# A streaming encoder layer on one core: two-input elementwise work of the input phase and of the up-projection's weights moved from GpSimd to VectorE, with a new table for the middle's steps

## The chip, the cores and the metric

The kernel runs on one core of a Trainium2 chip. The metric is the device time of one execution in microseconds (us), the median of several runs. Five engines work side by side, each taking its own queue of instructions in order: TensorE (PE; its weight loads are listed as PEld), VectorE (DVE), ScalarE (ACT), GpSimd (POOL) and SyncE (SP), which here only issues DMA transfers. ACT and POOL issue transfers as well, in order with their other instructions.

## The reference

One layer of a streaming encoder is computed for 1024 new prompt frames and 32 frames that continue an older stream, 1056 tokens with a model width of 1024, all in float32:

```python
proj = x @ prm['w_in']
q_lat, kv_lat, k_rope_raw, u, p_rwkv = jnp.split(proj, IN_SPLITS, axis=-1)
mla_out, ckv, krope = mla_mixer(q_lat, kv_lat, k_rope_raw, pos, ...)    # 6 heads, chunk-causal
s5_out, s5_state = s5_mixer(u, s5_x0, s5_block_len, prm)                 # 16 groups, 64 complex states
rwkv_out, rwkv_state, shift = rwkv_mixer(p_rwkv, shift0, rwkv_s0, prm)   # 6 heads of 64
merged = jnp.concatenate([mla_out, s5_out, rwkv_out], -1)
x = layer_norm(ALPHA * x + merged @ prm['w_out'], prm['ln1_g'], prm['ln1_b'])
hidden = jnp.square(jax.nn.relu(x @ prm['w_up']))                        # 4096 wide
x = layer_norm(ALPHA * x + hidden @ prm['w_down'], prm['ln2_g'], prm['ln2_b'])
```

RWKV mixes each token with the one before it, `p + (prev - p) * mu_shift`, ahead of everything else. Attention uses a rotary part of 32 dimensions, and S5 needs powers of a complex diagonal and products with its input and output matrices.

## The kernel before

**Split products.** Each float32 operand of a matrix product is split in two parts. ACT copies it to a rounded high part (L49), and another engine subtracts that from the operand, which leaves the low part, the residue (L50); both are in `split3`. `mm3` then does three products, high by high (L63), high by low (L65) and low by high (L67). The argument `lo_eng` of `split3` and `load3` names the engine of L50; without it, it is VectorE.

**Input phase** (0 to about 283 us). The projection goes in tiles of 128 columns. `load_w` loads the 128x1024 weights of a tile and splits them (`wmraw`, `wmhi`, `wmlo`). For the RWKV columns, `raw_in` has ACT copy the projected tile out of PSUM to `raw`, with GpSimd filling the borders (L222 to L224, L229, L230); `mixed` then makes the token shift: a subtraction of neighbours (L238) and a multiply-add on VectorE (L239). `stage_mixed` passes the shifted tile on, for q = 0 after a product with cumulated decays (helper at L344), otherwise by a DMA that ACT issues; `stage_lora` does the same for its tile (L249 is the issue) and splits the activated tile (`lact`, `lah`, `lal`). `stage_s5_params` computes powers and the products `cl`, `bl`, `tb` (L514 to L531); L538 on PE transposes `bl`, and ACT's copies of L539 follow it. `front_k` normalises and scales the keys of three pairs of heads (L383 to L394, with products at L342, L344 and one with `at` at L388) and hands them to a set of small products and transposes (L727 to L740). `rwkv_inv` makes a triangular inverse in steps on VectorE (L761, L762). `stage_kr` makes the rotary key (L162 to L164); `stage_q` takes the query's products out of PSUM on ACT (L1161), and `attn_setup` prepares tiles for the attention, among others four 32x1056 areas set to zero (L1111).

**Middle** (about 283 to 720 us). Four streams of steps are recorded in turn: F (scores and row maxima), O (exponentials and the product with the values), S (the RWKV scan) and X (S5). Which stream records its next step is read from `PLAN`, a string of 527 letters. Steps keep this order on PE.

**Output projection and first layer norm** (about 700 to 805 us), then the **MLP**. The up-projection (about 805 to 1160) uses seven products of halves in place of eight for each of 16 blocks of weights: sums of weight quarters (`ws`, L1609 and, for the first two blocks, L1762) are split by `operand` into 128x512 parts (`wo`), and sums of the activations (`xr`, `xt`, L1723) into `xo`. VectorE adds the results out of PSUM (L1634). The down-projection (about 1160 to 1450) loads the hidden layer back and splits it on VectorE and ACT.

**What sets the order.** The code is recorded in program order; a scheduler then orders each engine's instructions by a simulated timeline, in which priorities and the table above hold. So where an instruction changes its engine, its place among the others, and theirs, is set anew.

Of the kernel before, what the change touches and what calls it, by code (L numbers as in the profile page):

```python
# [11 lines left out]
ALU = mybir.AluOpType  # L12
# [84 lines left out]
def load_w(g, src, tag, cols):  # L97

    pool = g.wpools.get(tag, g.wpool)
    raw, hi, lo = (pool.tile([P, cols], dt, tag=t, name=tag + x, bufs=n)  # L100
                   for x, dt, (t, n) in zip(("raw", "hi", "lo"), (F32, F32R, F32R), g.wtags.get(tag, ((tag, WB),) * 3)))
    load3(g, src, raw, hi, lo, g.nc.gpsimd)
    return hi, lo


# [46 lines left out]
def stage_kr(g):  # L152

    nc = g.nc
    rope = g.p1.tile([P, T], F32, tag="f", name="ropek", bufs=5)[0:64]
    nc.sync.dma_start(out=rope, in_=g.a["rope"][0:64])
    kc = g.p1.tile([P, T], F32, tag="f", name="krc", bufs=5)
    t = g.p1.tile([P, T], F32, tag="f", name="krt", bufs=5)
    ps = in_proj(g, g.a["w_kr"], "wm", 64)
    for b, (s, n) in enumerate(BLK):  # L160
        nc.scalar.activation(out=kc[0:64, s:s + n], in_=ps[b][0:64, :n], func=AF.Copy)
    nc.gpsimd.tensor_tensor(out=t[0:32], in0=kc[32:64], in1=rope[32:64], op=ALU.mult)  # L162
    nc.gpsimd.tensor_tensor(out=kc[0:32], in0=kc[0:32], in1=rope[0:32], op=ALU.mult)
# [70 lines left out]
def mixed(g, raw, mtile):  # L234

    nc = g.nc
    mix = g.rawp.tile([P, WSH], F32, tag="mix", name="mix", bufs=2)
    nc.gpsimd.tensor_tensor(out=mix, in0=raw[:, 0:WSH], in1=raw[:, 1:WSH + 1], op=ALU.subtract)  # L238
    nc.vector.scalar_tensor_tensor(out=mix, in0=mix, scalar=g.vec[:, V_MU + mtile:V_MU + mtile + 1], in1=raw[:, 1:WSH + 1], op0=ALU.mult, op1=ALU.add)  # L239
    return mix  # L240


def stage_mixed(g, p, q, after=None, w=None):

    mix = mixed(g, raw_in(g, 4 + 3 * p + q, 3 * q + p, after, w), 3 * q + p)
    if q == 0:
        front_tools(g, p)[1](mix, mix, g.cs65[:, p], 1, 4, eng=g.nc.gpsimd)
    else:
        g.nc.scalar.dma_start(out=g.rw_d[p][:, 3] if q == 2 else g.mx_d[p], in_=mix)  # L249

# [6 lines left out]
def stage_lora(g):  # L257

    nc = g.nc
    mix = g.lmix  # L260
    act = g.lq.tile([P, WSH], F32, tag="lact", name="lact", bufs=1)
    g.table = [nc.scalar.activation(out=act[0:32], in_=mix[0:32], func=AF.Tanh)]
    nc.scalar.activation(out=act[32:64], in_=mix[32:64], func=AF.Copy)
    g.table.append(nc.scalar.activation(out=act[64:128], in_=mix[64:128], func=AF.Sigmoid))
    ah = g.lq.tile([P, WSH], F32R, tag="lah", name="lah", bufs=1)
    al = g.lq.tile([P, WSH], F32R, tag="lal", name="lal", bufs=1)
    split3(g, act, ah, al, nc.gpsimd)
    wl = g.lq.tile([P, 384], F32, tag="wl", name="wl", bufs=1)
# [12 lines left out]
    for p in PAIRS:
        cs = slice(p * P, p * P + P)
        nc.gpsimd.memset(g.cs65[:, p, 0:1040].rearrange("p (c x) -> p c x", x=65)[:, :, 0:1], 0.0)
        nc.gpsimd.memset(g.cs65[:, p, 1040:1041], 0.0)
        nc.gpsimd.memset(g.at[:, p, 1024:1026], 0.0)
        for s, n in runs:
            pool, tag = ((g.pfs, "fs"), (g.pt, "pt"))[i % 2]
            i += 1
            w, a = (pool.tile([P, 512], F32, tag=tag, name=tag)[:, :n] for _ in range(2))
            low(w, slice(0, 32), s, n)  # L290
            low(a, slice(32, 64), s, n)
            g.table.append(nc.scalar.activation(out=g.at[:, p, s:s + n], in_=a, func=AF.Sigmoid, bias=g.vec[:, V_A0 + p:V_A0 + p + 1]))
            out, w = (g.cs65[:, p, 1041:1073], w) if n == 32 else (chunk65(g.cs65[:, p], s // 64, n // 64, 1), w.rearrange("p (c x) -> p c x", x=64))
            g.table.append(nc.scalar.activation(out=out, in_=w, func=AF.Sigmoid, bias=g.vec[:, V_W0 + p:V_W0 + p + 1]))
    for p in PAIRS:
        cs = slice(p * P, p * P + P)
        gt = g.lq.tile([P, WSH], F32, tag="o", name="gt", bufs=2)
        nc.gpsimd.memset(gt[:, 1024:1026], 0.0)
        for s, n in runs:
            pool, tag = ((g.pfs, "fs"), (g.pt, "pt"))[i % 2]  # L300
            i += 1
            gate = pool.tile([P, 512], F32, tag=tag, name=tag)[:, :n]
            mm = low(gate, slice(64, 128), s, n)
            nc.vector.tensor_copy(out=gt[:, s:s + n], in_=gate)
        nc.sync.dma_start(out=g.rw_d[p][:, 5, :], in_=gt)
    g.last_lora = mm.ins
# [57 lines left out]
def front_k(g, p):  # L364
# [42 lines left out]
def bc(ap, shape):  # L407
    return ap.broadcast_to(shape)


def stage_s5_params(g, sp):
# [88 lines left out]
    def v4(t):  # L500
        return t[:, :2048].rearrange("p (g l c) -> p g l c", l=L5, c=16)
# [24 lines left out]
    for j in range(7):  # L526
        s3j = [P, G5, 16]
        l = 6 - j
        V.tensor_tensor(out=blv[:, :, j], in0=bbv[0], in1=bc(pr[:, :, l:l + 1], s3j), op=ALU.mult)
        nc.gpsimd.tensor_tensor(out=tbv[:, :, j], in0=bbv[1], in1=bc(pis[:, :, l:l + 1], s3j), op=ALU.mult)  # L530
    V.tensor_tensor(out=blv[:, :, 0:7], in0=blv[:, :, 0:7], in1=tbv[:, :, 0:7], op=ALU.add)  # L531
    V.tensor_copy(out=blv[:, :, 7], in_=bbv[0])
    yield
# [555 lines left out]
def attn_setup(g):  # L1089
# [16 lines left out]
    for i in range(NKT):  # L1106
        for ks in (g.kh, g.kl):
            if i:
                nc.gpsimd.tensor_copy(out=ks[i][64:128], in_=ks[0][64:128])
        for x in g.q2[i] if i < 2 else ():  # L1110
            nc.gpsimd.tensor_tensor(out=x[96:128], in0=g.ckv[96:128], in1=g.ckv[96:128], op=ALU.subtract)  # L1111
# [211 lines left out]
def middle(g, scan):  # L1323
# [36 lines left out]


PLAN = (
    "FFFFFFFFFFFSFFFFSFFFFFFFSFFFFFSFFFFSOOOSOFSOOOSFOOSOOOOSFSSOSOOFOOFSOOSXFOOOSFFOOOOSXOOFOOFSSOSSSOSO"
    "OFFXFXFOSOFOSSXFFFFOOSOSFOSXOSSFSOSOFOFSXOOSOFOSXOSOFOSOFOOXOFOSFSXOOOFSFOSOOOXFSOOSFOSOOXFSOOSFFFFS"
    "FXSFFFFSFFXSOOSFOSOOFSOOOOXFSXSSOOFOSOOSOFXOOSOOOFOSXOSFSOOOSFOOSXOOOOSFOSOXSFOOFXSSSFFFFFFSFSOOXSOS"
    "FFXSSOOFOSOOOSOOXOSOOOOOFSFOOSXSOOFOOOSSXFOSOFSFOFXOOSOFSOSOOFXOOOSSFOFSXFFFSFFFSFFFXSFSFFFSXOOFOSOO"
    "SOOSXSOOFOFSOSXOOFOSOFSOXOSOSFOXSOOOFOSOOOOFSSOSOXFSOOOSFOXFOOSOXSOOSFSSFFFFSFFFOOOOOSOOSOSOOOSOOOSS"
    "OOSSOOSOSOFOOSOOOOOOOOOOOOO"
)


# [1024 lines left out]
```

## Time and profile before

| | |
|---|---|
| median of 3 runs | 1492.15 us (1492.04 to 1496.15) |
| profiled execution, its time | 1493.61 us |
| its span, first to last instruction | 1491.8 us |
| mean granted clock of PE | 0.967 |
| PE busy | 1393.6 us (93%) |
| DVE busy | 960.8 us (64%) |
| ACT busy | 638.5 us (43%) |
| POOL busy | 419.3 us (28%) |

The profile shows one execution. An engine's busy share is a mean over stages that differ much, so times are read by stage: a table of windows gives each engine's busy time in a stretch, and the granted clock of PE in it (1.00 is full speed). A list of waits names, for an engine's idle time, the instruction that ended it. The chain that ended last is followed back from the last instruction, at each step to what released it. A row of a group gives busy us, mean ns of one instruction, and the idle time just before them. All times in windows and timelines count from the span's start.

### The profile page before, as it was taken

Reading aid. Unit: us, or ns where it says so; the run is one execution under the profiler, and the core shown is the slowest. Engines: PE = TensorE matmul, PEld = TensorE weight load, DVE = VectorE, ACT = ScalarE, POOL = GpSimd, SP = SyncE. Lnnn points to the kernel's source line nnn. Section 1 sums busy time; section 2 is a strip of 40 time slices with the busy share of each in tenths; the row PEclk is TensorE's granted clock in tenths of the full one; section 3 lists DMA queues with packets and bytes.
Section 4 is the critical chain, followed back from the end, with each engine's and each line's share of the span. In section 5 each row is a group of like instructions: output and inputs, shape, how many; then the busy total and the mean of one; then the engine's idle time right before and its main releaser. Section 6 shows DMA issues by size and latency. Waiting matters only on the chain.

```text
span 1491.8 us, 28327 instructions
## 1 busy us (share of the span) xinstructions
PE 1393.6 (93%) x11527; PEld 1245.1 (83%) x11527; DVE 960.8 (64%) x1594; ACT 638.5 (43%) x1122; POOL 419.3 (28%) x447
## 2 busy tenths in 40 slices
PE   7899989789999989979899899999999999999996
PEld 6889879567767656656588899999999999999996
DVE  8566859955566745454757875555556687675476
ACT  4434543414645654443324454444445433434332
POOL 3813581511111110121541644444440000000023
PEclk9999999979999999989999899999999999999998
DMA  5234363564343230132543353434428886354231
GB/s 198 88 117 175 102 204 88 144 136 94 90 104 77 79 83 23 40 97 83 185 144 121 100 187 135 156 132 143 159 102 322 305 284 189 102 157 141 68 99 75
DMA packets 150326, 198.59 MB, mean 133 GB/s; under 512 B 53392, under 2 KB 98116, under 8 KB 149688
## 3 DMA queue, kind: packets, MB, share of 16 engines
q1 hardware_dynamic: 129396, 175.91, 37.1%
q10 hardware_dynamic: 20448, 19.88, 4.3%
q8 instruction: 90, 1.47, 0.4%
q0 software_dynamic: 352, 1.01, 0.2%
q14 instruction: 40, 0.33, 0.1%
HBM read 129.42 MB, written 67.28 MB: 132 GB/s over the span
## 4 chain that ended last, share of the span: by engine, by line
PE 70%; DVE 12%; DMA 5%; issue 4%; ACT 4%; POOL 2%; SPq 1%; ACTq 0%; DVEq 0%; POOLq 0%
PE acc L63 17%; PE acc L65 17%; PE acc L67 17%; PE av L1256 3%; DVE y L762 2%; DVE tmp L761 1%; DMA wo<-in_w_out 1%; DMA mraw<-mg_d 1%; PE sc L63 1%; PE st L63 1%; PE st L65 1%; DVE mx L1227 1%; PE st L67 1%; PE prw L883 1%; PE scv L1138 1%
## 5 line engine op out<-in xcount | busy, mean ns | idle before, releaser
L63 PE MATMUL acc<-xo,wo 128*128 128x272 f32 (+1 forms) x896 | 256.3, 287 | 7.3 <-ACT wo L49 5.5
L67 PE MATMUL acc<-xo,wo 128*128 128x256 f32 (+1 forms) x896 | 254.2, 285 | 1.1 <-POOL wo L50 1.1
L65 PE MATMUL acc<-xo,wo 128*128 128x272 f32 (+1 forms) x896 | 254.6, 285 | 0.0
L67 PE MATMUL acc<-hop,wo 128*128 128x272 f32 (+1 forms) x896 | 193.9, 283 | 0.0
L63 PEld LDWEIGHTS acc<-xo,wo 128*128 128x128 f32 x896 | 169.7, 189 | 8.4 <-ACT wo L49 5.9
L67 PEld LDWEIGHTS acc<-xo,wo 128*128 128x128 f32 x896 | 169.4, 190 | 1.3 <-POOL wo L50 1.3
L65 PEld LDWEIGHTS acc<-xo,wo 128*128 128x128 f32 x896 | 170.0, 190 | 0.0
L65 PE MATMUL acc<-hop,wo 128*128 128x272 f32 (+1 forms) x768 | 158.6, 284 | 0.0
L63 PE MATMUL acc<-hop,wo 128*128 128x256 f32 (+1 forms) x768 | 158.3, 284 | 0.0
L67 PEld LDWEIGHTS acc<-hop,wo 128*128 128x128 f32 x896 | 142.7, 188 | 0.0
L63 PE MATMUL acc<-xh,wmhi 128*128 128x384 f32 (+3 forms) x384 | 129.0, 336 | 8.8 <-ACT xh L49 8.0
L65 PE MATMUL acc<-xl,wmhi 128*128 128x384 f32 (+3 forms) x384 | 128.7, 335 | 2.3 <-DVE xl L50 2.1
L67 PE MATMUL acc<-xh,wmlo 128*128 128x384 f32 (+3 forms) x384 | 128.5, 335 | 0.0
L65 PEld LDWEIGHTS acc<-hop,wo 128*128 128x128 f32 x768 | 119.2, 188 | 0.0
L63 PEld LDWEIGHTS acc<-hop,wo 128*128 128x128 f32 x768 | 118.1, 188 | 0.0
L50 POOL TENSOR_TENSOR wo<-ws,wo 128x512 fp32r<-128x512 f32 x64 | 89.6, 1402 | 98.6 <-ACT wo L49 97.4
L2134 POOL TENSOR_TENSOR wr<-wr,gb 128x512 f32<-128x512 f32 (+1 forms) x14 | 19.8, 1436 | 338.3 <-ACT wr L2132 327.2
L49 ACT ACTIVATE wo<-wr 128x512 fp32r<-128x512 f32 (+1 forms) x64 | 47.0, 739 | 119.4 <-PE acc L67 69.9
L50 POOL TENSOR_TENSOR wo<-wr,wo 128x512 fp32r<-128x512 f32 x48 | 66.1, 1380 | 92.7 <-ACT wo L49 92.7
L1256 PE MATMUL av<-ptk,vo 128*128 128x512 f32 (+5 forms) x204 | 75.6, 456 | 12.3 <-POOL ptk L1283 5.6
L1634 DVE TENSOR_TENSOR hx<-acc,u 128x272 f32<-128x272 f32 (+1 forms) x96 | 40.8, 428 | 71.4 <-PE acc L67 71.3
L63 PEld LDWEIGHTS acc<-xh,wmhi 128*128 128x128 f32 (+1 forms) x384 | 72.5, 189 | 12.2 <-ACT xh L49 8.3
(545 smaller groups left out, 3296.2 us busy)
## 6 DMA issues: line engine op xcount, KB each, us to landing
hraw<-h_d SPq DMA_DIRECT2D x48, 528.0 KB, 3.7
wr<-in_w_up SPq DMA_DIRECT2D x35, 512.0 KB, 3.7
h_d<-hx SPq DMA_DIRECT2D x16, 792.0 KB, 3.3
h_d<-ht SPq DMA_DIRECT2D x16, 792.0 KB, 9.6
wd<-in_w_dn SPq DMA_DIRECT2D x16, 512.0 KB, 9.1
wr<-in_w_dn SPq DMA_DIRECT2D x16, 512.0 KB, 5.2
ld<-rw SPq DMA_DIRECT2D x24, 320.0 KB, 4.6
wmraw<-in_w_m SPq DMA_DIRECT2D x12, 512.0 KB, 4.7
```

The source lines that it names most:

```text
L49: nc.scalar.activation(out=hi, in_=ps, func=AF.Copy)
L50: (lo_eng or nc.vector).tensor_tensor(out=lo, in0=ps, in1=hi.bitcast(F32), op=ALU.subtract)
L63: nc.tensor.matmul(out=outs[i], lhsT=lh, rhs=rhs[i][0], start=start, stop=False, **kw)
L65: nc.tensor.matmul(out=outs[i], lhsT=lh, rhs=rhs[i][1], start=False, stop=False, **kw)
L67: nc.tensor.matmul(out=outs[i], lhsT=ll, rhs=rhs[i][0], start=False, stop=stop, **kw)
L761: V.tensor_tensor(out=tv, in0=bc(y[:, :, 0:m, s:s + 1], [H, 2, m, n]), in1=bc(nn[:, :, s:s + 1, s + 1:32], [H, 2, m, n]), op=ALU.mult)
L762: V.tensor_tensor(out=y[:, :, 0:m, s + 1:32], in0=y[:, :, 0:m, s + 1:32], in1=tv, op=ALU.add)
L883: nc.tensor.matmul(out=pw[hsl(c), p - p0, h], lhsT=g.xt[p][hsl(c), t, h], rhs=r[hsl(c), p, K_A:K_NV + 1:K_NV, h], start=True, stop=True)
L1138: nc.tensor.matmul(out=ps[:n, j], lhsT=c, rhs=g.wkv[:, 1, p * P:p * P + P], start=True, stop=True)
L1256: nc.tensor.matmul(out=po[:, c:n], lhsT=vo[:w, kt].rearrange("p a x -> p (a x)")[:, 64 * i:64 * i + P], rhs=pt[:w, c:n], start=kt == tiles ...
L1634: V.tensor_tensor(out=to(c), in0=st.bank[key, c], in1=other(c), op=ALU.add)
L2134: nc.gpsimd.tensor_tensor(out=o[:n, c], in0=o[:n, c], in1=g.gb2[:n, 0, c], op=ALU.mult)
```

## The change

GpSimd's instructions with two inputs in the input phase and for the weights of the up-projection become VectorE's: the residue of each projection weight, of the LoRA tile and of each operand of the up-projection, the subtraction of the token shift, the product of `stage_mixed`, the product at L388, the three of the rotary key and the two lines of S5. The four areas set to zero at L1111, a subtraction of a tile from itself on GpSimd, become a copy by ACT with scale 0. The table of the middle has the same letters in the same numbers (217 O, 140 F, 132 S, 38 X), many of them a few places off. GpSimd keeps the borders of `raw`, its memsets, casts and transfers, and its part of the middle and of the other stages.

```diff
@@ load_w
-    load3(g, src, raw, hi, lo, g.nc.gpsimd)
+    load3(g, src, raw, hi, lo)
@@ stage_kr
-    nc.gpsimd.tensor_tensor(out=t[0:32], in0=kc[32:64], in1=rope[32:64], op=ALU.mult)
-    nc.gpsimd.tensor_tensor(out=kc[0:32], in0=kc[0:32], in1=rope[0:32], op=ALU.mult)
-    nc.gpsimd.tensor_tensor(out=kc[0:32], in0=kc[0:32], in1=t[0:32], op=ALU.add)
+    nc.vector.tensor_tensor(out=t[0:32], in0=kc[32:64], in1=rope[32:64], op=ALU.mult)
+    nc.vector.tensor_tensor(out=kc[0:32], in0=kc[0:32], in1=rope[0:32], op=ALU.mult)
+    nc.vector.tensor_tensor(out=kc[0:32], in0=kc[0:32], in1=t[0:32], op=ALU.add)
@@ mixed
-    nc.gpsimd.tensor_tensor(out=mix, in0=raw[:, 0:WSH], in1=raw[:, 1:WSH + 1], op=ALU.subtract)
+    nc.vector.tensor_tensor(out=mix, in0=raw[:, 0:WSH], in1=raw[:, 1:WSH + 1], op=ALU.subtract)
@@ stage_mixed
-        front_tools(g, p)[1](mix, mix, g.cs65[:, p], 1, 4, eng=g.nc.gpsimd)
+        front_tools(g, p)[1](mix, mix, g.cs65[:, p], 1, 4, eng=g.nc.vector)
@@ stage_lora
-    split3(g, act, ah, al, nc.gpsimd)
+    split3(g, act, ah, al)
@@ front_k
-    nc.gpsimd.tensor_tensor(out=kk, in0=kk, in1=a, op=ALU.mult)
+    nc.vector.tensor_tensor(out=kk, in0=kk, in1=a, op=ALU.mult)
@@ stage_s5_params
-    nc.gpsimd.tensor_tensor(out=v4(tb), in0=bc(csw[:, :, None, :], s4), in1=bc(pis[:, :, :, None], s4), op=ALU.mult)
+    nc.vector.tensor_tensor(out=v4(tb), in0=bc(csw[:, :, None, :], s4), in1=bc(pis[:, :, :, None], s4), op=ALU.mult)
-        nc.gpsimd.tensor_tensor(out=tbv[:, :, j], in0=bbv[1], in1=bc(pis[:, :, l:l + 1], s3j), op=ALU.mult)
+        nc.vector.tensor_tensor(out=tbv[:, :, j], in0=bbv[1], in1=bc(pis[:, :, l:l + 1], s3j), op=ALU.mult)
@@ attn_setup
-            nc.gpsimd.tensor_tensor(out=x[96:128], in0=g.ckv[96:128], in1=g.ckv[96:128], op=ALU.subtract)
+            nc.scalar.activation(out=x[96:128], in_=g.ckv[96:128], func=AF.Copy, scale=0.0)
@@ PLAN (first of its six rows)
-    "FFFFFFFFFFFSFFFFSFFFFFFFSFFFFFSFFFFSOOOSOFSOOOSFOOSOOOOSFSSOSOOFOOFSOOSXFOOOSFFOOOOSXOOFOOFSSOSSSOSO"
+    "FFFFFFFFFFFSFFFFFFSFFFFFFSFFFFSFFFFSOOOSOFSOOOSFOOSOOOOSFSSOSFOOOOFSOOSXFOOOSFOOSXOOOOFFOOOSFSSSOSSO"
...
@@ operand
-    split3(g, src, w[:, 0], w[:, 1], g.nc.gpsimd)
+    split3(g, src, w[:, 0], w[:, 1])
```

What this does to the order of the queues is shown at three places; a row names the line, the operation, output and inputs, and the shape.

The first is on VectorE in the input phase, where the third token shift of the first stretch (L239) and the S5 product `bl` (L531) are made. Before:

```order
L239 SCALAR_TENSOR_TENSOR mix<-mix,vec,raw 128x1058
L597 TENSOR_TENSOR u_94<-u_94,nrm 128x32
L516 TENSOR_TENSOR cl<-cl,tb 128x2048
L521 TENSOR_SCALAR pis<-pi,sgn 128x128
L239 SCALAR_TENSOR_TENSOR mix<-mix,vec,raw 128x1058
L531 TENSOR_TENSOR bl<-bl,tb 128x16x7x16
L239 SCALAR_TENSOR_TENSOR mix<-mix,vec,raw 128x1058 x2
```

The same place now, with `wmlo` the residue of a projection weight and `lal` that of the LoRA tile:

```order
L50 TENSOR_TENSOR wmlo<-wmraw,wmhi 128x1024
L238 TENSOR_TENSOR mix<-raw 128x1058
L565 COPY a_219<-w_753 128x16
L567 COPY u_94<-a_219 128x16
L530 TENSOR_TENSOR tb<-bb,pis 128x256 x7
L50 TENSOR_TENSOR lal<-lact,lah 128x1058
L239 SCALAR_TENSOR_TENSOR mix<-mix,vec,raw 128x1058
L566 TENSOR_SCALAR u_94<-a_219,sgn 128x16
L531 TENSOR_TENSOR bl<-bl,tb 128x16x7x16
L238 TENSOR_TENSOR mix<-raw 128x1058
```

What stood in GpSimd's queue (the residues, L238, L530) stands between VectorE's own instructions, and L516 has moved ahead of this piece.

The second is on ACT at the end of the input phase, among the query's copies out of PSUM (`scq`). Before:

```order
L1161 ACTIVATE qrope<-scq 128x384 x2
L1161 ACTIVATE qturn<-scq 128x384
L1161 ACTIVATE qrope<-scq 128x288
L1161 ACTIVATE qturn<-scq 128x384
L1079 ACTIVATE cpast<-sct 128x512
```

The same place now:

```order
L1161 ACTIVATE qrope<-scq 128x384 x2
L1161 ACTIVATE qturn<-scq 128x384
L1111 ACTIVATE qh<-ckv 32x1056
L1111 ACTIVATE ql<-ckv 32x1056
L1111 ACTIVATE qh<-ckv 32x1056
L1111 ACTIVATE ql<-ckv 32x1056
L1161 ACTIVATE qturn<-scq 128x384
L1161 ACTIVATE qrope<-scq 128x288
```

The four zeroings stand together between two of the copies.

The third is on VectorE at the start of the up-projection, up to the last of the weight sums of the first two blocks (`ws<-ws,wr`) and the first sum out of PSUM (`u<-acc,u`). Before:

```order
L50 TENSOR_TENSOR xo<-xt,xo 128x4x256
L1723 TENSOR_TENSOR xt<-xr,xt 128x1088
L1762 TENSOR_TENSOR ws<-wr 128x512
L1723 TENSOR_TENSOR xt<-xr,xt 128x1024
L1762 TENSOR_TENSOR ws<-wr,ws 128x512
L1762 TENSOR_TENSOR ws<-ws,wr 128x512
L50 TENSOR_TENSOR xo<-xt,xo 128x4x272
L1634 TENSOR_TENSOR u<-acc,u 128x272
```

The same place now, where `wo` are residues of weights:

```order
L50 TENSOR_TENSOR xo<-xt,xo 128x4x256
L1723 TENSOR_TENSOR xt<-xr,xt 128x1088
L50 TENSOR_TENSOR wo<-ws,wo 128x512 x3
L1723 TENSOR_TENSOR xt<-xr,xt 128x1024
L50 TENSOR_TENSOR wo<-wr,wo 128x512 x2
L1762 TENSOR_TENSOR ws<-wr,ws 128x512
L1762 TENSOR_TENSOR ws<-ws,wr 128x512
L1634 TENSOR_TENSOR u<-acc,u 128x272
```

Five residues stand in this piece ahead of the last sum; five more stand ahead of it earlier in the queue, and the residue `xo` of the activations has moved behind `u`.

More of the change, by code (lines that the diff above doesn't have):

```diff
@@ L1362 @@
 PLAN = (
-    "FFFFFFFFFFFSFFFFSFFFFFFFSFFFFFSFFFFSOOOSOFSOOOSFOOSOOOOSFSSOSOOFOOFSOOSXFOOOSFFOOOOSXOOFOOFSSOSSSOSO"
[L1364 to L1368, printed above, removed]
+    "FFFFFFFFFFFSFFFFFFSFFFFFFSFFFFSFFFFSOOOSOFSOOOSFOOSOOOOSFSSOSFOOOOFSOOSXFOOOSFOOSXOOOOFFOOOSFSSSOSSO"
+    "OFFXXFOSFOFOSSXFFFFOOSOSSFOSXOOSFSFSOOFSXOOSOFOSXOSFOOSOOFOFXOXOSFSOOOFSFFOOSOOXSSOOOFSOOXFSFOOSFFFS"
+    "FXSFFFFSFFXSOOSFOSOOFSOOOOXFSSSOOXFOSOOSFXOOSOOOFOOSXOSSOFOOFOSOSXOOOOSFOSOXOFFSOXSFFSSFFFSFFSOOXSOS"
+    "FFXSSFOSOOOOOSOOXOSOOOFOOSFOOSXSFOOOOOSSXFOSFFOOSFOOSXOFSOOSFXOOOOSSFOFSXFFFSFFFSFFFXSFSFFFSOXOFOOSO"
+    "SOOSOXOSFFOSOSOXOFSOOFSOOXOSSXOSOOOOFOFOOOSFSSSOXSOFOOOSFOXFOXOSOSOOSFSSFFFFSFFFOOOOOOSOOSOOSOOOSOSS"
+    "OOSSSOOSOFOSOOOOOOOOOOOOOOO"
 )
```

## The prediction

> **What bounds the kernel now.** The page comes first: its span and its busy times.
>
> ```profile
> span 1491.8 us, 28327 instructions
> PE 1393.6 (93%) x11527; PEld 1245.1 (83%) x11527; DVE 960.8 (64%) x1594; ACT 638.5 (43%) x1122; POOL 419.3 (28%) x447
> ```
>
> TensorE (PE) is busy 93% of the span, so the change can be worth something only where PE is not running, or runs at half clock. GpSimd (POOL), which loses work here, has 28%. The table of windows tells the stages apart. Its columns are the window, its length, the busy time of PE, PEld, VectorE (DVE), ScalarE (ACT) and POOL, the granted clock, the DMA share and GB/s.
>
> ```profile
> 31.00:69.00 38.00, 36.61 (x226) 35.13 (x224) 25.24 (x28) 13.32 (x21) 32.27 (x27) 1.00 0.24 84
> 73.30:76.60 3.30, 3.30 (x13) 3.08 (x11) 1.26 (x1) 1.91 (x5) 2.00 (x2) 0.50 0.73 209
> 182.50:189.20 6.70, 5.79 (x79) 5.26 (x80) 6.67 (x7) 4.34 (x8) 1.53 (x2) 0.50 0.73 172
> 298.60:315.50 16.90, 13.70 (x96) 10.18 (x96) 8.78 (x22) 1.37 (x3) 5.18 (x6) 0.50 0.88 198
> 300.00:725.00 425.00, 381.69 (x4030) 285.47 (x4029) 232.93 (x505) 190.91 (x398) 63.26 (x129) 0.93 0.33 87
> 834.50:844.60 10.10, 7.22 (x31) 6.93 (x32) 10.10 (x11) 2.68 (x5) 8.36 (x5) 0.50 0.47 158
> 850.00:1150.00 300.00, 300.00 (x2476) 300.00 (x2476) 174.24 (x277) 136.56 (x199) 122.93 (x94) 1.00 0.44 161
> 1200.00:1250.00 50.00, 50.00 (x414) 50.00 (x413) 41.94 (x42) 20.74 (x26) 0.00 (x0) 1.00 0.81 269
> ```
>
> In the up-projection (850 to 1150) PE is busy 300 of 300 us at full clock: nothing there can get shorter. In the input phase POOL works 32.27 us out of 38, and there, around 300 and around 840, the granted clock falls to 0.50 after PE has stood still. Work done in such a window takes twice its time, so a window that goes is worth at most half its length.
>
> Next, the groups of instructions: the moved forms on POOL, and like forms on DVE, ACT for the zeroing. The columns are count, total busy time, mean ns of one, then idle time before them.
>
> ```profile
> L50 POOL TENSOR_TENSOR wo<-ws,wo 128x512 fp32r<-128x512 f32 x64 | 89.6, 1402 | 98.6 <-ACT wo L49 97.4 <-PE acc L67 1.3
> L50 POOL TENSOR_TENSOR wmlo<-wmraw,wmhi 128x1024 fp32r<-128x1024 f32 x14 | 34.9, 2490 | 45.0 <-ACT wmhi L49 44.6 <-POOL kpast L1103 0.4
> L50 DVE TENSOR_TENSOR wo<-wr,wo 128x1024 fp32r<-128x1024 f32 x16 | 19.6, 1224 | 15.0 <-ACT wo L49 15.0
> L1206 ACT ACTIVATE qh<-kh 32x1056 fp32r<-32x1056 f32 x4 | 4.3, 1079 | 0.1
> ```
>
> The same subtraction of 128x1024 takes 2490 ns on POOL and 1224 on DVE: about 1.2 ns for each element of a row. From that I estimate 1.27 us for a 1058-wide operation on DVE, 2.3 for 2048, 0.65 for 512 and 0.4 for 256.
>
> **Part by part. The first stall (T1, 55 to 77 us).** Waits, the chain that ended last, and DVE's timeline:
>
> ```profile
> PE pt L538 <- ACT em L539: 2.6, 1, 2.6
> PE pt L538 <- DVE bl L531: 1.2, 1, 1.2
> ```
>
> ```profile
> 57.37 2.40 POOL lal L50
> ...
> 59.84 3.55 POOL raw L224
> 63.39 2.32 POOL wmlo L50
> ...
> 69.24 0.33 ACTq L249
> ...
> 71.63 1.15 PE pt L538 x8
> ```
>
> ```profile
> 52.11 1.69 DVE L239 SCALAR_TENSOR_TENSOR mix<-mix,vec,raw 128x1058 f32<-128x1058 f32 x1 [4.45 <-POOL mix L238]
> 57.40 5.96 DVE L531 TENSOR_TENSOR bl<-bl,tb 128x1792 f32<-128x1792 f32 x1 [3.60 <-POOL tb L530]
> 67.89 1.32 DVE L239 SCALAR_TENSOR_TENSOR mix<-mix,vec,raw 128x1058 f32<-128x1058 f32 x1 [4.52 <-POOL mix L238]
> ```
>
> The third token shift of this stretch (L238, then L239 on DVE) comes last in POOL's row of work, and DVE starts its half only at 67.89. ACT can't issue the DMA of that tile (L249) before, and the copy of L539, for which PE waits, stands behind that issue in ACT's queue. L531 (5.96 us from 57.40) and the one-column copy of L224 (3.55 from 59.84) lie beside each other: the copy has next to nothing to do and waits for L531, which itself waits for lal. The Trainium skill, page "SBUF — State Buffer", section "Who interferes with whom", says that a DVE instruction with two SBUF inputs and a GpSimd one that reads SBUF exclude each other for the whole instruction, and these two rows agree.
>
> Between 50.2 and 67.9 DVE now has L239 (1.7), two L238 (2.5), seven L530 (2.8), lal (1.3), L531 alone (1792 wide, 2.0), one wmlo (1.2): 11.5 us for what took 17.7 us. The third shift ends some 6 us sooner, more than the longer wait. Both waits go: 1.2 + 2.6 = 3.8, and the half-clock window of 3.3 us behind them (73.3 to 76.6), half of it 1.7. T1 = -5.5, and 0 if the shifted tile's input arrives late.
>
> **The second stall (T2, 158 to 189).** Here the chain is DVE's own, the first two pairs of RWKV in front_k. The waits, then DVE's timeline:
>
> ```profile
> ACT kk L731 <- DVE f L344: 5.2, 1, 5.2
> PE pti L733 <- ACT kk L734: 3.3, 1, 3.3
> ```
>
> ```profile
> 158.54 2.21 DVE L90 SCALAR_TENSOR_TENSOR fc<-fc,fq 128x1058 f32<-128x1058 f32 x1 [0.57 <-ACT fc L89]
> ...
> 161.05 2.89 DVE L91 SCALAR_TENSOR_TENSOR kk<-fc,kk 128x1058 f32<-128x1058 f32 x1
> ...
> 169.78 3.06 DVE L91 SCALAR_TENSOR_TENSOR kk<-f,kk 128x1058 f32<-128x1058 f32 x1
> ...
> 175.60 2.35 DVE L394 SCALAR_TENSOR_TENSOR at<-at,f 128x1058 f32<-128x1058 f32 x1
> ...
> 179.12 3.18 DVE L344 TENSOR_TENSOR f<-at,cs 128x1024 f32<-128x1024 f32 x2
> ```
>
> Against 1.27 for each (1.6 for the last pair) these five lose 0.9 + 1.6 + 1.8 + 1.1 + 1.6 = 7.0 us beside POOL. Put in are one L388 (1.27), a 1024 and a 512 weight residue (1.2 + 0.65) and one L238 (1.27), 4.4 us; two small L342 (1.35) stand behind f now. Net, f is done 7.0 - 4.4 + 1.35 = 4.0 us sooner, where PE waited 3.3. T2 = -3.3, and half of the 6.7 us window, -3.4: -6.7. It holds by a narrow margin; the other end is 0.
>
> **Entry to the middle (T3, 265 to 299) and the zeroing (T4).**
>
> ```profile
> 269.96 2.07 DVE L761 TENSOR_TENSOR tmp<-y,nn 108x270 f32<-108x270 f32 x1
> ...
> 274.17 0.39 DVE L761 TENSOR_TENSOR tmp<-y,nn 108x224 f32<-108x224 f32 x1
> ```
>
> ```profile
> 269.55 2.18 POOL L1111 TENSOR_TENSOR qh<-ckv 32x1056 fp32r<-32x1056 f32 x1
> ```
>
> ```profile
> PE sc L63 <- DVE kl L50: 3.7, 2, 3.1
> ...
> PE scq L1160 <- ACT qnope L1161: 3.0, 1, 3.0
> ```
>
> The inverse's steps take 2.07 beside POOL's L1111 and some 0.4 to 0.45 without. Four such pairs give DVE 4 x 1.65 = 6.6 us. The two long waits behind it, 3.1 and 3.0, are shorter than that: T3 = -6.1, other end 0 (transfers set them). T4: ACT takes the four zeroings, 4 x 1.08 = 4.3 us, which stand among the evacuations of the query's PSUM tiles. PE pays between 0 (spare PSUM tiles carry it) and 4.3 + 1.7 for a half-clock window as at 73; I take the middle, +3.0.
>
> **From output projection to up-projection (T6, 805 to 845).** Timeline of DVE, chain, and waits:
>
> ```profile
> 808.99 2.38 DVE L1723 TENSOR_TENSOR xt<-xr 128x1088 f32<-128x1088 f32 x1
> ...
> 815.78 0.68 DVE L1762 TENSOR_TENSOR ws<-wr 128x512 f32<-128x512 f32 x1
> ```
>
> ```profile
> 832.52 3.43 DVE ws L1762 x2
> ```
>
> ```profile
> PE acc L63 <- ACT wo L49: 5.5, 2, 4.5
> ```
>
> DVE runs without a gap, and PE waits for its last sum of weights (ends 835.9). Nine operations of DVE stand beside POOL's residues there, from this L1723 to the two sums in the chain's row; each loses about what the first does, 2.38 - 1.3 = 1.1 us: 9.7 in all. Ten residues of 512 come in ahead of that sum, 10 x 0.68 = 6.8. Net T6 = -2.9, between +2 (three residues more on the path) and -9.6 (wait gone, with half of the 10.1 us window).
>
> **The rest.** In the up-projection 112 residues go to DVE: 112 x 0.68 = 76 us on its 174.24 of 300, so 250 at the most, hidden under PE's 300 of 300; T7 = 0. If that cover is gone, see the third rival. At the very start (0 to 30 us) a wmlo of 1.2 us stands ahead of other residues, and POOL no longer collides with the S5 parameters: 0, within -1 and +1.2. The new table reorders the middle, 425 us of which PE is busy 381.69. No row prices one place in it. Work and count per stream are the same, so T8 = 0; as ends I take three stalls of the size above either way, +-10.
>
> **Sum.** -5.5 - 6.7 - 6.1 + 3.0 - 2.9 = -18.2 us. The profiled execution took 1493.61 (span 1491.8), 1.46 above the median 1492.15. So 1493.6 - 18.2 - 1.5 = 1473.9.
>
> **Rivals.** *Both windows go (chance 0.13).* If PE's gaps around 298 and 836 fall short enough, the half-clock windows of 16.9 and 10.1 us go too: 8.5 + 5.1 = 13.6 more, 1460. For it: these are the two longest windows near changed work. Against: between 299 and 316 the chain of waits holds transfers that the change leaves alone.
>
> *An exchange without gain (0.12).* POOL's work is put on the engine that it slowed. In the input phase 14 wmlo x 1.22, ten L238, three L388 and a lal x 1.27, L515 (2.3), L530 (2.8), three L344 (1.6 each) and three 32-row products (1.27) make 49 us more for DVE, of which the rows above win back 4.0 (L531), 7.0 (T2) and 6.6 (T3). If the added instructions stand ahead of the urgent ones in DVE's queue, T1, T2 and T3 are lost and the time is 1492. For it: in T2 the margin is 0.7 us. Against: before T1 DVE is idle for 4.45 + 3.60 + 4.52 = 12.6 us because of POOL, and idle time takes the added work free of charge. The Trainium skill, page "Perfetto Trace Analysis", section "Optimizing Scalar/DVE Operations", says that shifting work between GpSimd and DVE might not help, since they share a port. By that rule the sum is near 0, while by the rows above it is -18, because POOL's instructions take twice as long as DVE's for the same data and block both engines for it.
>
> *DVE's queue in the up-projection (0.11), slower.* POOL waited 98.6 us, nearly all for ACT, before 64 of its 112 residues, 1.5 each. In DVE's queue such a wait also holds the sums of PSUM tiles (L1634) behind it, which PE needs. If one residue in seven is not covered, one for each of the 16 weight blocks, 16 x 1.5 = 24.6 us come on top: 1493.6 - 18.2 + 24.6 - 1.5 = 1498.5. It turns the sign from 1.1 us for each of the 16 weight blocks (18.2 / 16). For it: DVE would be at 250 of 300 there. Against: in the down-projection DVE does the weights' residues already, is at 41.94 of 50, waits for ACT (15.0 us in the row of 16 above), and PE still has 50.00.
>
> **How the numbers follow.** The forecast has what is left, 0.64. Its own ends: T2 and T3 lost give -18.2 + 12.8 = -5.4, 1486.7; a better table gives 1464. About 0.3% (4.5 us) can be told from no change. Forecast and first rival are faster: 0.64 + 0.13 = 0.77; same 0.12; slower 0.11. The second rival spreads over 1487 to 1495, about half of it on either side of 1490; the first reaches 1457 where T4 costs nothing. The range, 1457 to 1490, leaves out the third rival (0.11), half of the second (0.06) and a gain of the table on top of the first (0.03).
>
> **What would show it.** Right: no PE wait on L538 and L733 above 1 us and full clock at 73 and 182; DVE's L531 about 2 us, L761 at 270 wide about 0.45; PE still 300 of 300 in the up-projection. Wrong: PE waiting for L1634's tiles in the up-projection, for L1161 behind the zeroing, or longer in the middle, 300 to 725, with DVE no busier.

## The result, and the profile after

The changed kernel takes 1467.74 us (median of 4 runs, 1466.29 to 1473.35) against 1493.38 for the kernel before in the same comparison: a ratio of 0.9833, 95% interval 0.9801 to 0.9865, or 25 us less. The forecast was 1473.9, range 1457 to 1490. The profiled execution took 1466.29, the fastest of the four, so its trace flatters the kernel by about 1.5 us. An extract of the page after:

```profile
span 1464.5 us, 28210 instructions
...
PE 1376.6 (94%) x11527; PEld 1237.8 (85%) x11527; DVE 986.2 (67%) x1752; ACT 643.6 (44%) x1126; POOL 186.5 (13%) x285
```

POOL lost 233 us of work, DVE gained only 25. The groups of DVE after show why; the columns are count, busy time, mean ns, idle time before. The last row is one of DVE's own sums in the kernel before:

```profile
L50 DVE TENSOR_TENSOR wo<-ws,wo 128x512 fp32r<-128x512 f32 x64 | 43.4, 682 | 3.6 <-ACT wo L49 3.6
L50 DVE TENSOR_TENSOR wo<-wr,wo 128x512 fp32r<-128x512 f32 x48 | 32.7, 687 | 25.1 <-ACT wo L49 25.0
L1609 DVE TENSOR_TENSOR ws<-wr 128x512 f32<-128x512 f32 x28 | 19.1, 680 | 0.0
L50 DVE TENSOR_TENSOR wmlo<-wmraw,wmhi 128x1024 fp32r<-128x1024 f32 x14 | 17.0, 1217 | 6.2 <-ACT wmhi L49 6.0
```

```profile
L1609 DVE TENSOR_TENSOR ws<-wr 128x512 f32<-128x512 f32 x28 | 30.9, 1107 | 1.9 <-POOL wo L50 1.0
```

What took POOL 1402 and 2490 ns takes DVE 682 and 1217, and DVE's own sums are shorter too, 680 ns in place of 1107. The windows after (window, length, busy PE, PEld, DVE, ACT, POOL, clock) stand against those of before, shifted by what had been won by then:

```profile
66.00:76.00 10.00, 10.00 (x97) 8.72 (x96) 1.08 (x2) 4.50 (x10) 0.41 (x5) 1.00 0.49 200
168.00:182.00 14.00, 14.00 (x146) 12.15 (x144) 13.97 (x17) 8.69 (x15) 3.06 (x3) 1.00 0.77 223
273.90:287.60 13.70, 5.93 (x18) 4.66 (x18) 5.54 (x15) 3.20 (x8) 2.59 (x2) 0.50 0.84 228
278.00:705.00 427.00, 378.30 (x4034) 286.08 (x4035) 236.11 (x512) 193.40 (x402) 64.80 (x131) 0.94 0.34 90
813.20:816.60 3.40, 3.40 (x18) 3.40 (x17) 3.40 (x7) 0.33 (x1) 0.00 (x0) 0.50 0.58 210
830.00:1130.00 300.00, 300.00 (x2476) 300.00 (x2476) 198.51 (x360) 136.69 (x198) 0.00 (x0) 1.00 0.46 168
```

The first two half-clock windows are gone: PE is busy all the time, at full clock, around 70 and 175. At the entry to the middle (273.9) there is a long one, at the entry to the up-projection one of 3.4 us in place of 10.1. The up-projection is full, as it was.

PE's instructions give landmarks. The table has their starts in both traces, and the gain of each stretch between. Each trace is of one execution, so the gains add up to 27.2 us and not to 25:

| landmark on PE | before | after | gain in the stretch |
|---|---|---|---|
| first L548 (first stretch done) | 78.1 | 69.8 | 8.3 |
| last product of the projections (L67 on wmlo) | 263.3 | 245.0 | 10.0 |
| first L1256 (the middle runs) | 332.1 | 310.6 | 3.2 |
| first product of the up-projection (xo) | 800.6 | 779.6 | -0.5 |
| first product of the down-projection (hop) | 1140.7 | 1113.4 | 6.2 |
| last product | 1478.7 | 1451.5 | 0.0 |

### The profile page after: what moved, and what is told of

Read it like the earlier page. It is cut to its first block, busy times and chain, and to the rows that moved or that the text cites. A ratio compares the mean times of both kernels' runs of the same rounds, so it can differ in the third digit from the quotient of the medians.

```text
span 1464.5 us, 28210 instructions
## 1 busy us (share of the span) xinstructions
PE 1376.6 (94%) x11527; PEld 1237.8 (85%) x11527; DVE 986.2 (67%) x1752; ACT 643.6 (44%) x1126; POOL 186.5 (13%) x285
## 4 chain that ended last, share of the span: by engine, by line
PE 79%; DVE 8%; DMA 5%; ACT 3%; issue 2%; SPq 1%; ACTq 0%; POOL 0%; DVEq 0%; POOLq 0%
PE acc L63 20%; PE acc L65 20%; PE acc L67 19%; PE av L1256 3%; PE st L65 1%; PE st L63 1%; PE st L67 1%; DVE mx L1227 1%; PE prw L883 1%; PE sc L63 1%; PE scv L1138 1%; DMA xr<-in_xt 1%; DMA mraw<-mg_d 1%; PE prt L841 1%; DMA wr<-in_w_up 1%
## 5 line engine op out<-in xcount | busy, mean ns | idle before, releaser
L67 PE MATMUL acc<-xo,wo 128*128 128x256 f32 (+1 forms) x896 | 253.9, 285 | 1.9 <-DVE wo L50 1.9
L67 PE MATMUL acc<-hop,wo 128*128 128x272 f32 (+1 forms) x896 | 193.9, 283 | 0.0
L67 PEld LDWEIGHTS acc<-xo,wo 128*128 128x128 f32 x896 | 168.8, 189 | 2.3 <-DVE wo L50 2.3
L67 PEld LDWEIGHTS acc<-hop,wo 128*128 128x128 f32 x896 | 142.7, 188 | 0.0
L67 PE MATMUL acc<-xh,wmlo 128*128 128x384 f32 (+3 forms) x384 | 126.1, 328 | 0.0
L1256 PE MATMUL av<-ptk,vo 128*128 128x512 f32 (+5 forms) x204 | 74.9, 453 | 14.0 <-ACT po L1261 9.3
L63 PEld LDWEIGHTS acc<-xh,wmhi 128*128 128x128 f32 (+1 forms) x384 | 71.3, 186 | 10.6 <-ACT xh L49 8.3
L50 DVE TENSOR_TENSOR hop<-hraw,hop 128x1056 fp32r<-128x1056 f32 (+3 forms) x58 | 70.4, 1213 | 14.3 <-ACT hop L49 14.2
L50 DVE TENSOR_TENSOR wo<-wr,wo 128x512 fp32r<-128x512 f32 (+1 forms) x64 | 52.3, 820 | 39.4 <-ACT wo L49 39.4
L65 PEld LDWEIGHTS acc<-xl,wmhi 128*128 128x128 f32 (+1 forms) x384 | 71.4, 186 | 7.2 <-DVE xl L50 3.9
```

Of the source, the lines that this page charges most:

```text
L50: (lo_eng or nc.vector).tensor_tensor(out=lo, in0=ps, in1=hi.bitcast(F32), op=ALU.subtract)
L63: nc.tensor.matmul(out=outs[i], lhsT=lh, rhs=rhs[i][0], start=start, stop=False, **kw)
L65: nc.tensor.matmul(out=outs[i], lhsT=lh, rhs=rhs[i][1], start=False, stop=False, **kw)
L67: nc.tensor.matmul(out=outs[i], lhsT=ll, rhs=rhs[i][0], start=False, stop=stop, **kw)
L1256: nc.tensor.matmul(out=po[:, c:n], lhsT=vo[:w, kt].rearrange("p a x -> p (a x)")[:, 64 * i:64 * i + P], rhs=pt[:w, c:n], start=kt == tiles ...
```

## The experiments

Each ran beside the kernel before, on the same chip as it; there were three such comparisons. The median of the kernel before was 1494.77 us for e1 to e4, 1496.95 for e5, e6, e7 and e9, and 1495.13 for e8 and e11 to e13, so ratios are compared, and where a ratio is turned into us that median is used.

**The parts.** e1 has only the last edit of the change (`operand`) in the kernel before. e2 has all the others without the new table. e3 is the whole change with the old table, e4 the new table alone.

```diff
e1, in before:
-    split3(g, src, w[:, 0], w[:, 1], g.nc.gpsimd)
+    split3(g, src, w[:, 0], w[:, 1])
e2, in after (and PLAN of before):
-    split3(g, src, w[:, 0], w[:, 1])
+    split3(g, src, w[:, 0], w[:, 1], g.nc.gpsimd)
e3, in after: PLAN of before
e4, in before: PLAN of after
```

> Only the residues of the up-projection's 112 weight operands go to VectorE; the rest of the kernel, its table too, is that of before. Theory (GpSimd's and VectorE's two-input work hold each other up, and the gain lies where VectorE sets the end): the entry to the up-projection gets some 6 us shorter, as the landmarks of the two traces show (-21.0 us at the first product of the up-projection, -27.2 at its last), the rest of the up-projection stays at PE 300 of 300: about 1487. Rival (residues wait in VectorE's queue): slower than before, 1495 or more, with PE waits on L1634. Rival (the entry gets its gain from the earlier start of VectorE after the input phase): no change, 1493.

> The input phase's part alone (projection weights, token shift, LoRA, keys, rotary key, S5, and the zeroing on ACT), with the residues of the up-projection on GpSimd and the table of before. Theory: the 21 us of the input phase, 1472. Rival (the new table carries much of it): 1480 or more.

> The whole change with the table of before. Theory: the table is worth nothing measurable (the landmarks lose 0.9 us between 299 and the output projection), 1467 with 4 us either way. Rival (the table was made to fit the new costs and without it the streams stall): 1475 or more.

> The new table alone in the kernel of before. Theory: 1493 with 4 us either way. Rival (the table carries the gain): 1485 or less. If the table only fits the new costs: 1500 or more.

| | median us | ratio to before, 95% interval | about us |
|---|---|---|---|
| whole change | 1467.74 | 0.9833 (0.9801 to 0.9865) | -25 |
| e1, up-projection alone | 1492.34 | 0.9982 (0.9965 to 0.9998) | -2.7 |
| e2, input phase alone | 1471.52 | 0.9848 (0.9811 to 0.9884) | -22.7 |
| e3, whole, old table | 1472.87 | 0.9850 (0.9821 to 0.9879) | -22.4 |
| e4, new table alone | 1490.92 | 0.9972 (0.9952 to 0.9991) | -4.2 |

The input phase carries the gain. The up-projection's part brings 2.7 us, less than the 6 that were expected, though its stretch on PE is 4.3 us shorter in the profiled run (3.9 more came off the middle in that run, which was the fastest of its ten, and the input phase lost 2.8). It isn't slower: DVE took the residues and PE stayed full, as this window of e1 shows (columns as above).

```profile
845.00:1130.00 285.00, 285.00 (x2354) 285.00 (x2353) 187.32 (x353) 125.54 (x189) 0.00 (x0) 1.00 0.42 149
```

The table alone is worth 4.2 us (interval 1.3 to 7.2); inside the whole change it can't be told from nothing, since the intervals of e3 and the whole overlap. In e4's trace the last product starts 5.6 us sooner: 0.4 lost up to the first L1256, 5.9 won from there on, where the table rules or behind it.

**What slows VectorE.** e11 and e12 add work to GpSimd that nobody reads, at the same places, in the kernel after: e11 reads two inputs, e12 only writes.

```diff
e11, in after, behind L239:
+    dm = g.rawp.tile([P, 384], F32, tag="dm", name="dm", bufs=1)
+    [nc.gpsimd.tensor_tensor(out=dm, in0=raw[:, 0:384], in1=raw[:, 1:385], op=ALU.subtract) for _ in range(4)]
e12, the same with, in place of the second line:
+    [nc.gpsimd.memset(dm, 0.0) for _ in range(10)]
```

> The kernel after with 40 two-input subtractions of 128x384 more on GpSimd, four behind each token shift, into a tile that nobody reads: some 42 us of GpSimd's time by the 1.1 us of like instructions in the trace of before. Nobody waits for them. Theory (GpSimd reading and VectorE's two-input work shut each other out): VectorE's instructions beside them grow from 0.5 to 1.3 us to about twice that, and the input phase loses 5 to 15 us: 1472 to 1482. Rival (what counted was only that slow GpSimd instructions stood on the path): 1467, durations on VectorE as in after.

> The kernel after with 100 memsets of 128x384 more on GpSimd at the same places (about as much of GpSimd's time, writing only, nothing read), into a tile that nobody reads. Theory: writing alone does not hold VectorE up, 1467 and VectorE's durations as in after. Rival (any work of GpSimd holds VectorE up, or delays GpSimd's own border copies): 1472 or more, as with the subtractions.

e11: 1482.82 us, 0.9917 (0.9892 to 0.9942), 12.4 us less than before; e12: 1473.29, 0.9857 (0.9835 to 0.9879), 21.4 less. Like amounts of GpSimd's time cost 9 us more when they read. In the traces the projections end 7.0 us sooner than before in e11, 16.3 in e12 and 18.3 in the whole change. The groups of GpSimd and of DVE in e11:

```profile
L239 POOL TENSOR_TENSOR dm<-raw 128x384 f32<-128x384 f32 x40 | 51.4, 1285 | 21.9 <-ACT raw L225 17.0 <-DVE nrm L594 2.9
L224 POOL COPY raw<-vec 128x1 f32<-128x1 f32 x10 | 12.1, 1206 | 0.0
...
L530 DVE TENSOR_TENSOR tb<-bb,pis 128x256 f32<-128x256 f32 x7 | 5.8, 982 | 0.0
```

and in e12:

```profile
L239 POOL MEMSET dm<- 128x384 f32 x100 | 42.2, 422 | 5.2
L224 POOL COPY raw<-vec 128x1 f32<-128x1 f32 x10 | 4.4, 444 | 0.0
...
L530 DVE TENSOR_TENSOR tb<-bb,pis 128x256 f32<-128x256 f32 x7 | 3.8, 723 | 0.0
```

The seven small products of L530 take 718 ns in after and 723 beside 42 us of memsets, but 982 beside subtractions. So reading is what holds VectorE up, as the theory has it. e12's time lies in its rival's range (1472 or more), but its interval overlaps with that of the whole change, and VectorE's durations are those of after. The 982 of e11 is a mean of two kinds; the row of this line has the least, the median and the greatest of the seven:

```profile
L530 DVE TENSOR_TENSOR tb<-bb,pis x7: 643/1201/1240, 50.8 to 55.4; 128x256 f32<-128x256 f32 x7
```

Four of them took about twice their time, as expected, and three took no longer than in after. A part of e11's loss goes another way: the added subtractions wait in GpSimd's queue, most of all for ACT's copies of `raw` (17.0 of 21.9 us), and the border copies of the next `raw` stand behind them. Two waits of e11 between 30 and 80 us, of a kind that after does not have there:

```profile
ACT raw L225 <- POOL raw L222: 4.3, 1, 4.3
...
PE acc L63 <- ACT raw L225: 2.4, 1, 2.4
```

How e11's loss divides between the two was not measured.

**The second stall by itself.** e9 is the kernel before with L388 on VectorE.

```diff
-    nc.gpsimd.tensor_tensor(out=kk, in0=kk, in1=a, op=ALU.mult)
+    nc.vector.tensor_tensor(out=kk, in0=kk, in1=a, op=ALU.mult)
```

> The kernel before, with the product of L388 alone on VectorE (three instructions). Theory: these three hold up five of VectorE's in front_k; without them PE's wait on L733 of 3.3 us and the 6.7 us at half clock behind it go, T2 = -6.7: 1487. Rival (the chain is set by the amount of VectorE's work, and three more take back what they give): 1493.

1500.61 us, ratio 1.0034 (1.0007 to 1.0062): a little slower, where 6.7 us less had been expected. The profiled run took 1493.36, the fastest of ten (up to 1507.13), so the trace doesn't show what makes the others slow; their granted clock is lower, 0.957 to 0.968 against 0.969 here. VectorE's timeline in e9:

```profile
171.99 1.25 DVE L91 SCALAR_TENSOR_TENSOR kk<-f,kk 128x1058 f32<-128x1058 f32 x1
...
179.58 1.34 DVE L344 TENSOR_TENSOR f<-at,cs 128x1024 f32<-128x1024 f32 x2
...
192.20 3.73 DVE L344 TENSOR_TENSOR y<-kk,cs 128x1024 f32<-128x1024 f32 x2
```

The rows of 3.06 and 3.18 us before are now 1.25 and 1.34, PE's wait at 180 is down to 0.5, and the clock there is full:

```profile
180.00:190.00 10.00, 8.80 (x114) 7.55 (x113) 10.00 (x12) 4.47 (x8) 4.38 (x4) 1.00 0.73 221
195.00:203.00 8.00, 5.52 (x42) 4.08 (x34) 4.28 (x4) 3.37 (x7) 3.56 (x4) 0.79 0.72 230
```

But the third pair is held up instead (3.73 us), PE waits 2.5 us for it at 195, and a half-clock window follows. In this run the wait has moved on by one pair: beside the 3.73 stands another of GpSimd's instructions with two inputs (L344, 193.2 to 196.1). In the whole change, which takes these off GpSimd too, the waits on L733 are gone.

**The entry to the middle.** e5 puts the zeroing of L1111 back on GpSimd in the kernel after; e6 moves only this zeroing in the kernel before. e7 and e13 shorten the way of the first query head in the kernel after.

```diff
e5, in after (e6 the other way round, in before):
-            nc.scalar.activation(out=x[96:128], in_=g.ckv[96:128], func=AF.Copy, scale=0.0)
+            nc.gpsimd.tensor_tensor(out=x[96:128], in0=g.ckv[96:128], in1=g.ckv[96:128], op=ALU.subtract)
e7, in after (L2248 and L2249 likewise on nc.sync):
-            nc.scalar.dma_start(out=g.q_d[2 * p + h, 0:64], in_=q[hsl(h)])
+            nc.sync.dma_start(out=g.q_d[2 * p + h, 0:64], in_=q[hsl(h)])
e13, in after (L2247 as a VectorE copy, L2248 and L2249 on nc.gpsimd):
+            (nc.gpsimd if p else nc.scalar).dma_start(out=g.q_d[2 * p + h, 0:64], in_=q[hsl(h)])
-        nc.gpsimd.dma_start(out=g.q_d[h, 64:96], in_=qa[32 * h:32 * h + 32])
+        nc.sync.dma_start(out=g.q_d[h, 64:96], in_=qa[32 * h:32 * h + 32])
```

> The kernel after, with the four zeroings of L1111 back on GpSimd. By the prediction's terms the entry to the middle loses T3 and wins T4, -6.1 + 3.0 undone: 3 us slower than after, 1471. Rival (the wait at the entry is set by ACT's queue, which the zeroings burden): some 4 us faster than after, 1463.

> The kernel before, with the four zeroings of L1111 on ACT and nothing else changed. By the prediction's terms T3 + T4 = -3.1: 1490. Rival (the waits at the entry to the middle hang on ACT's issues and on transfers, and VectorE's earlier end there brings nothing): 1493, or some us slower by ACT's 4.3 us.

> The kernel after, with the DMAs that write the query's parts to q_d (L1173) and the two of the shift state (L2248, L2249) issued by SP in place of ACT; PE's order is that of after. In the trace of after, PE stands still from 270.0 to 281.7 while ACT issues them in 3.2, 1.5 and 3.2 us ahead of the copies that PE's next scores need. Theory: most of the 11.5 us goes, and with it part of the 13.7 us at half clock: 1456 to 1461. Rival (the transfers are queued anyway, SP's own queue only takes over the wait): 1467, or slower if the inverse's transfers stand behind them on SP.

> The kernel after, with the first query head's way to PE made shorter: its rotary part goes to q_d from SP (L1187) and not behind GpSimd's casts of 8.4 us, the other heads' parts (L1173 of the second and third pair) and the shift state (L2247 to L2249) leave ACT's queue for GpSimd and VectorE. Theory: PE's gap of 11.5 us at 270 shrinks by 5 to 9 us and some of the half-clock time behind it goes: 1457 to 1463. Rival (the keys' copies or the transfers' own time set the end): 1467.

| | median us | ratio, 95% interval |
|---|---|---|
| e5, zeroing back on GpSimd | 1469.38 | 0.9823 (0.9794 to 0.9852) |
| e6, zeroing alone on ACT | 1490.87 | 0.9959 (0.9941 to 0.9978) |
| e7, issues on SP | 1470.20 | 0.9831 (0.9795 to 0.9868) |
| e13, the first head's way shorter | 1469.87 | 0.9836 (0.9816 to 0.9857) |

e5, e7 and e13 can't be told from the whole change (0.9833). The waits of after show what the entry hangs on:

```profile
PE sc L63 <- DVE kl L50: 11.4, 1, 11.4
...
ACT qnope L1161 <- issue: 4.9, 1, 4.9
...
ACT kh L49 <- issue: 3.2, 1, 3.2
```

The two waits of some 3 us that T3 counted have become one of 11.4, which hangs on ACT's queue, where DMA issues (L1173, L2249) hold up the keys' copies. With these taken off ACT (e7), PE still waits 11.1, now for the query's transfer, which stands behind them in SP's queue:

```profile
PE sc L63 <- ACT qh L49: 11.1, 1, 11.1
```

In e13 the first score comes 4.6 us earlier than in after, and PE then waits at later steps:

```profile
PEld av L1256 <- POOL ptk L1283: 9.9, 2, 9.2
PE av L1256 <- POOL ptk L1283: 9.4, 2, 9.0
...
PE sc L63 <- DVE mx L1227: 7.4, 3, 6.2
```

Each way to shorten this wait gave another in its place. In the profiled runs the stretch from the projections' end to the first L1256, and the one from there to the up-projection, gain in us: 3.2 and -0.5 (after), -0.6 and 0.5 (e5), 5.4 and -5.4 (e7), 7.8 and -7.2 (e13). What e7 and e13 win at the entry is gone by the end of the middle. That the middle takes it back isn't shown, though: e8 and e12, whose edits touch neither, read 2.1 and -3.0, and 3.7 and -6.3. The middles of after and e12 by themselves (columns as above):

```profile
310.60:779.60 469.00, 426.89 (x3920) 322.28 (x3920) 267.70 (x540) 213.23 (x459) 91.78 (x149) 0.96 0.32 89
312.00:786.90 474.90, 430.90 (x3920) 324.29 (x3920) 267.07 (x540) 213.43 (x459) 89.98 (x149) 0.94 0.32 88
```

PE, VectorE, ScalarE and GpSimd do the same instructions in the same order there, and e12 takes 5.9 us longer at a lower clock. So a single trace can't tell a loss of 5 to 7 us in the middle from the spread between runs, and what holds the middle's end was not found. e6 gained more than the 3.1 us that were expected, but not at its entry: in its trace it gains 2.4 us up to the first L1256 after losing 2.7 before it, and 2.0 in the middle. That is 2.0 in all at the last product, in a run of 1491.5 set against a run of before of 1493.6, while the median beside e6 was 1496.95. So where its 6 us (3.3 to 8.8) come from stays open.

**Behind the entry to the up-projection.** e8 gives the later blocks' residues back to GpSimd, in the kernel after (`operand` hands its third argument on to `split3`).

```diff
-    w.update({x: operand(g, made(x)) for x in [PROD[n][0] for n in order]})
+    w.update({x: operand(g, made(x), g.nc.gpsimd) for x in [PROD[n][0] for n in order]})
```

> The kernel after, with the residues of the up-projection's later blocks (those of up_sums) back on GpSimd; the first two blocks and the ones made ahead of time stay on VectorE. Theory: only the entry was worth something, behind it PE hides either engine's work: 1467, equal to after. Rival (the later blocks gain or lose by VectorE's queue): some 3 us to either side.

1471.10 us, 0.9852 (0.9822 to 0.9881): its interval overlaps with the whole change's, and its stretch of the up-projection is 5.7 us shorter than before, against 6.2. GpSimd is busy again, and PE is as full as in after:

```profile
830.00:1130.00 300.00, 300.00 (x2477) 300.00 (x2476) 173.08 (x273) 135.89 (x199) 121.76 (x93) 1.00 0.45 163
```

So no gain of the later blocks can be seen; these 5.7 us are won without them.

## Why the prediction was right, by its own steps

The direction and the range were right, and in T1, T2 and T6 the mechanism too, but the forecast lay 6 us above the measured time. In the traces each of these three terms is 2.8 to 3.3 us short; T3 and T4 came out right by luck.

**T1 (-5.5).** The stretch to the first L548 gained 8.3. Both waits and the half-clock window are gone. DVE's timeline after:

```profile
51.98 3.85 DVE L531 TENSOR_TENSOR bl<-bl,tb 128x1792 f32<-128x1792 f32 x1
55.75 1.24 DVE L238 TENSOR_TENSOR mix<-raw 128x1058 f32<-128x1058 f32 x1
56.92 1.21 DVE L50 TENSOR_TENSOR wmlo<-wmraw,wmhi 128x1024 fp32r<-128x1024 f32 x1
...
58.16 1.30 DVE L239 SCALAR_TENSOR_TENSOR mix<-mix,vec,raw 128x1058 f32<-128x1058 f32 x1
```

The third shift starts at 58.2 in place of 67.9, 9.7 us sooner where 6 were reckoned, although L531 takes 3.85 us and not the 2.0 that the prediction named as a sign (3.82 to 3.96 in all traces with the input phase's part, against 5.96 before). The first L538 starts at 60.2 against 63.4, 3.2 sooner, of which its own wait was only 1.2: some 2 us came off before it, at the start, where the prediction put 0.

**T2 (-6.7).** Right in its mechanism, short in size: the stretch from there to the end of the projections gained 10.0. The term counted the first of three waits on L733. The trace of before has, from 183 on:

```profile
PE pti L733 <- ACT kk L734: 5.7, 3, 3.3
PE pt L185 <- ACT rms L184: 1.3, 1, 1.3
```

After, no wait on L733 is left in the whole stretch, and 0.8 is left on L185: 5.7 + 0.5, and the 3.4 of the clock, make 9.6. e9 says that L388 alone would not have done it; of the 7.0 us of the working 3.4 stood beside it, the rest beside residues and L238.

**T3 + T4 (-6.1 + 3.0).** The sum, -3.1, met the trace (-3.2), but not by its reasons. L761 fell from 2.07 to 0.43 us as said; the two waits did not go but were gathered into one of 11.4. The stretch from the end of the projections to the first L1256, before and after:

```profile
263.30:332.10 68.80, 56.67 (x557) 39.97 (x556) 51.20 (x80) 20.74 (x44) 26.98 (x27) 0.83 0.59 143
245.00:310.60 65.60, 51.29 (x558) 37.04 (x556) 45.42 (x82) 25.08 (x51) 18.81 (x23) 0.87 0.65 150
```

PE stands still for 14.3 us after against 12.1 before, 2.2 more where 6.1 less were reckoned. Of what makes the stretch shorter, the clock is the part that can be named: half-clock windows of 17.1 us in place of 23.9, worth 3.4. The step that failed is "the two long waits are shorter than that": the gain of VectorE there was not the last thing that PE waited for. e5 does not settle it. Its zeroings hold the inverse up again, as in

```profile
253.94 2.02 DVE L761 TENSOR_TENSOR tmp<-y,nn 108x224 f32<-108x224 f32 x1
```

against 0.39 in after. In its trace the stretch is 3.8 us longer than in after, but the whole time can't be told from that of the whole change, and neither can the 3 us that were expected. T4's price was not paid: PE has no wait on L1161 in after, behind the four zeroings on ACT.

**T6 (-2.9).** Measured 6.2 in the profiled run. DVE's rows lost their excess as reckoned, and PE's waits at this place:

```profile
PE acc L63 <- ACT wo L49: 2.8, 1, 2.8
...
PE acc L67 <- DVE wo L50: 1.9, 2, 1.2
```

are 4.7 where 5.5 + 1.1 stood before, and three shorter waits of 1.8 in all are gone as well: 3.7 less. About as much is the clock: the window of 10.1 us shrank to 3.4, half of the difference 3.4 us, which the forecast kept for its range and the first rival. What the term lacked is most of all the clock. That rival came true for the most part at this place, not at the other: a long window remains at the entry to the middle.

**T7, T8 (0).** Right within what can be told. PE is 300 of 300 in the up-projection. VectorE waits for ACT there 3.6 + 25.1 = 28.7 us before 112 residues, 0.26 each against GpSimd's 1.5: they stand later in the queue, and the third rival (slower) had no ground; its trigger was 1.1 us for each of the 16 blocks. VectorE is busy 198.51 of 300 there, not 250, since its own sums got shorter. The table (T8) can't be told from nothing.

**The exchange without gain.** DVE's busy time grew by 25 us, with 49 us of new work in the input phase and 76 in the up-projection: some 100 us were won back. They were won where both engines had worked side by side: up to the projections' end VectorE's busy time went from 192.8 to 199.9 us, and in the up-projection's stretch from 213.8 to 235.9, while in the down-projection, where nothing was moved, it stayed at 229.0. The Trainium skill, page "Perfetto Trace Analysis", section "Optimizing Scalar/DVE Operations", says that shifting work between these two might not help. Had it not helped here, the time would have stayed near 1493; the measured 25 us say otherwise for this kernel. What the Trainium skill, page "SBUF — State Buffer", section "Who interferes with whom", says of readers and writers on GpSimd agrees with e11 and e12 (982 against 723 ns on average).

## What to carry to other kernels

Where GpSimd and VectorE both do two-input work, a move to VectorE costs it far less than its price list says, since it also loses the hold-ups: here 125 us of moved work added 25. But look for the place where this engine's end is what PE waits for. The same kind of move was worth 23 us in the input phase, which has such waits, and nothing that could be seen where PE was full. A stall that is followed by a half-clock window counts by half that window too, while a stall whose next releaser is as late is only moved.

## What the runs showed of the hardware

GpSimd's one-column copies (L224, L229) got slower when VectorE took the work: 1308 and 1500 ns each on average against 990 and 444 before, as they wait for VectorE's instructions. In e12 one such copy lasted over several of them in turn:

```profile
52.43 7.30 POOL L230 COPY shl<-raw 128x1 f32<-128x1 f32 x1
```

In that time VectorE did five instructions (L531, L238, a residue, a small one and L239). So in this row the reader on GpSimd did not wait for one instruction alone, but for as many as followed closely.

PE's half-clock windows last 3.4 us or multiples of it in the traces (3.4, 6.8, 10.2, 13.7), and the same gap does not always bring the same window. PE's wait of 2.6 us on L538 (69.0 to 71.6 before) is 2.6 in the traces of e1, e4, e6 and e9 too, whose edits don't touch this place. A window of 3.4 us follows it in before, e1 and e6 (from 73.2, 73.9 and 74.2), and one of 6.8 in e4 and e9 (from 71.5 and 71.3, while PE still waits). That of e9:

```profile
71.30:78.10 6.80, 6.50 (x25) 5.95 (x26) 1.32 (x1) 4.10 (x9) 4.25 (x7) 0.50 0.59 218
```

So one gap cost about half of 3.4 us or about half of 6.8. The runs of one kernel with one order differ by 7 us (1466.29 to 1473.35 for the change), and windows of different length are at least a part of such differences, as in the middles of after and e12. What decides between the two lengths was not tested.
